# An encoder layer on one core: a new emission order around the output projection

## The chip, the cores and the metric

The kernel runs on one core of one Trainium2 chip. The metric is the device time of one execution in microseconds (us), the median of several runs. Before the change it is 1085.55 us (three runs, 1084.59 to 1087.48).

## The reference, cut to what matters

```python
def hybrid_mixer(u, w_in, ..., w_out):
    qa, ka, va, ga, za, qs, ks, vs = jnp.split(u @ w_in, SPLITS, axis=-1)
    ...
    o_a = o_f + o_b                       # gated linear attention, 4 heads, two directions
    o_a = o_a * lax.rsqrt(jnp.mean(o_a * o_a, axis=-1, keepdims=True) + NORM_EPS)
    o_a = (o_a * gla_norm).reshape(B, L, 512) * jax.nn.silu(ga)     # the output gate
    o_s = banded_window_gqa(qs, ks, vs, sink, rel_table)            # 8 heads, |i-j| <= 128
    return jnp.concatenate([o_a, o_s], axis=-1) @ w_out             # the output projection

h = h + rmsnorm(hybrid_mixer(rmsnorm(h, g1), ...), g2)
h = h + rmsnorm(jnp.square(jax.nn.relu(rmsnorm(h, g3) @ w_up)) @ w_down, g4)
```

There are 1024 tokens of width 1024, all in float32, and the feed-forward width is 4096.

## The kernel before, in words

Products are built from a high and a low part of each float32 factor (three matmuls hi*hi, lo*hi, hi*lo), so TensorE does most of the work. Each weight tile is loaded as float32 (`raw`, two buffers), cast to its high part by ScalarE (L93), and VectorE subtracts to get the low part (L196).

The program is a list of steps. The string ORDER is split into tokens, and a loop emits the instructions of one step per token. The framework then schedules: from the emission order, which acts as priority, it makes a fixed instruction list for each engine and each DMA queue and puts semaphore waits in. An engine executes its list strictly in that order. Moving a token therefore moves instructions on all lists, and a waiting instruction holds whatever stands behind it.

The steps that matter here are these.

- `gHh`, a gate step (`ga_half`, `proj_ga`): the gate of linear-attention head H for token half h. TensorE does 24 matmuls into the bank `pin` (L222: `uth,wh` x8, `uth,wl` x8, `utl,wh` x8), ScalarE takes the silu (L647, which needs another activation table than the exp of the attention), VectorE multiplies with the head's output (L649; that output `otr` is loaded by L648 on ScalarE's queue), and SyncE's queue stores four blocks into `otd` of the four tiles of that half (L651). A head's weights are fetched when the head before it in the list is done, so one head's two halves share one fetch.
- `S`, one attention step (`swa_step`) of 16; step u handles a block of 128 queries for one of two key heads. TensorE transposes the four heads' probabilities (`ppt`, L171), computes the next step's logits (`pl`, L545 and L546) and multiplies with the values (`pvo`, L579 to L583). VectorE casts and splits each transpose (L95, L571), adds the bias and takes a minimum on each logits bank (L548), then scales (L562). ScalarE does the exp (L551), and the copy of `pvo` (L585) that VectorE's L586 completes. Steps 2n and 2n+1 complete `otd` of tile n. `pl` and `pvo` share two banks of PSUM; so do `ppt` and `pzt` below.
- `Wk`, `wk` (`fetch_wo`): load, cast and split the k-th 128 rows of w_out (L752 for k < 4, in two halves by L756 for k >= 4; L93; L196).
- `Mn` (`wout_mm`): the output projection of tile n (128 tokens). It loads `otd[n]` (L801), casts (L802), splits (L803) and does 48 matmuls into two banks `pm` (L810: 32 with the high part of the activations, L815: 16 with the low part).
- `Nn` (`wout_norm`): squares of `pm` (L823), the root on GpSimd (L180, L181), scaling (L830), the residual (L832; the row of x is loaded by L820 on ScalarE's queue), squares again (L835), the root, and the second scaling (L839) into the tile `tb`.
- `Tn` (`wout_tr`): eight transposes of `tb` (`pzt`, L171), copied out by ScalarE (L858, L860) and VectorE (L861).

The list of one attention step, since both parts of the change turn on it:

```python
def swa_step():
    ...
    if u + 1 < 16:
        units[u + 1].load()
    for i in range(4):
        units[u].trans(i)
        if u + 1 < 16:
            units[u + 1].logits(i)
    units[u].pv()
    if u + 1 < 16:
        units[u + 1].norm()
```

After the output projection come the feed-forward products (L994, then L1223) to the end of the kernel.

Of the kernel before, what the change touches and what calls it, by code (L numbers as in the profile page):

```python
# [20 lines left out]
S = 1024  # L21
# [51 lines left out]
ORDER = (  # L73
# [4 lines left out]
)  # L78


# [1227 lines left out]
```

## Time and profile before

| | |
|---|---|
| median of three runs | 1085.55 us |
| the profiled execution | 1088.56 us |
| its span, first to last instruction | 1086.8 us |
| TensorE busy | 1048.9 us, 97% |
| VectorE busy | 744.0 us, 68% |
| ScalarE busy | 525.5 us, 48% |
| mean share of the 16 DMA engines in use | SyncE's queue 32.2%, GpSimd's 11.6%, ScalarE's 5.1% |

The profile comes from one execution. Times in the views are us from the start of its span. A timeline row gives the start, the length, the engine, the line, the operation, `out<-in`, the shapes, a count, and in brackets the idle time ahead of it with what ended that. PEclk is the clock granted to TensorE, where 1.00 is 2.4 GHz and 0.50 is 1.2 GHz. Matmul rows overlap by their pipelining, so pitches are taken between starts.

### The profile page before, as it was taken

To read this page: it belongs to the slowest core of one execution; us is meant where nothing else is said; L and a number is where in the kernel's file an instruction comes from. 1 tells how busy PE (TensorE), PEld (TensorE's weight loads), DVE (VectorE), ACT (ScalarE), POOL (GpSimd) and SP (SyncE) were. 2 spreads that over 40 slices of the span, in tenths; PEclk is the share of its full clock that TensorE was granted. 3 is DMA by queue.
4 is the path that set the end of the run, shared out by engine and by line. 5 is a ranking of instruction groups with operands and counts; after the bars stand their busy time and mean duration, and the time that the engine had idled before them with its cause. 6 is when DMAs were issued, how large, how long until landed. Compare 5 with 4: busy or idle time off the path is not lost.

```text
span 1086.8 us, 13683 instructions
## 1 busy us (share of the span) xinstructions
PE 1048.9 (97%) x4950; PEld 858.0 (79%) x4950; DVE 744.0 (68%) x1165; ACT 525.5 (48%) x890; POOL 161.4 (15%) x246
## 2 busy tenths in 40 slices
PE   7999999999997999989999999999999999999996
PEld 5787788888885878768888888888778888888885
DVE  7659458799887767798665666564479764547564
ACT  5565324424766444466555555554444334345342
POOL 4211012111211111111221212112100000004002
PEclk9999999999998999999999999999999999999999
DMA  7355443613666432546563544537982333345522
GB/s 227 111 159 173 131 115 84 143 40 93 190 171 162 122 121 84 160 152 207 177 191 116 177 143 148 172 119 238 392 325 97 98 97 97 116 136 193 194 97 97
DMA packets 138805, 164.82 MB, mean 152 GB/s; under 512 B 17473, under 2 KB 94273, under 8 KB 138738
## 3 DMA queue, kind: packets, MB, share of 16 engines
q1 hardware_dynamic: 108626, 108.36, 32.2%
q0 software_dynamic: 22560, 37.76, 11.6%
q10 hardware_dynamic: 7552, 17.83, 5.1%
q8 instruction: 39, 0.64, 0.2%
q14 instruction: 28, 0.23, 0.1%
HBM read 111.47 MB, written 52.45 MB: 151 GB/s over the span
## 4 chain that ended last, share of the span: by engine, by line
PE 81%; DVE 9%; ACT 3%; issue 3%; DMA 3%; POOL 1%; SPq 0%; ACTq 0%; DVEq 0%; POOLq 0%
PE pa L994 16%; PE pa L1223 14%; PE pin L222 11%; PE pc L994 8%; PE pb L1223 6%; PE pc L1223 6%; PE pm L810 4%; PE pb L994 4%; PE pkv L222 2%; PE ppt L171 1%; PE pm L815 1%; PE pl L545 1%; DMA wd<-in_w_down_dram 1%; PE pkv L692 1%; PE pl L546 1%
## 5 line engine op out<-in xcount | busy, mean ns | idle before, releaser
L1223 PE MATMUL pa<-r 128*128 128x512 f32 x768 | 175.1, 389 | 0.8 <-DVE r L1163 0.8
L1223 PEld LDWEIGHTS pa<-r 128*128 128x128 f32 x768 | 144.0, 188 | 31.4 <-DVE r L1163 1.6
L1162 DVE TENSOR_TENSOR r<-ra,r 128x1024 fp32r<-128x1024 f32 x56 | 68.5, 1223 | 106.7 <-ACT r L1160 105.3
L1160 ACT CAST r<-ra 128x1024 fp32r<-128x1024 f32 x56 | 58.9, 1053 | 165.9 <-PE pa L1223 94.1
L994 PE MATMUL pa<-th,r 128*128 128x512 f32 x384 | 102.3, 389 | 0.7 <-ACT sn L1009 0.7
L994 PEld LDWEIGHTS pa<-th,r 128*128 128x128 f32 x384 | 72.0, 188 | 16.0 <-ACT sn L1009 1.1
L222 PE MATMUL pin<-uth,wh 128*128 128x512 f32 x256 | 70.9, 400 | 0.0
L1223 PE MATMUL pb<-r 128*128 128x512 f32 x288 | 69.7, 390 | 0.0
L222 PE MATMUL pin<-uth,wl 128*128 128x512 f32 x256 | 69.4, 396 | 0.0
L1223 PE MATMUL pc<-r 128*128 128x512 f32 x288 | 69.2, 389 | 0.0
L810 PE MATMUL pm<-wo,b 128*128 128x512 f32 x256 | 67.5, 403 | 1.5 <-ACT b L802 1.5
L222 PE MATMUL pin<-utl,wh 128*128 128x512 f32 x256 | 66.9, 392 | 0.0
L1163 DVE TENSOR_TENSOR r<-wd,r 128x1024 fp32r<-128x1024 f32 x52 | 63.4, 1219 | 3.8 <-ACT r L1161 3.8
L1223 PEld LDWEIGHTS pb<-r 128*128 128x128 f32 x288 | 53.9, 188 | 11.9 <-DVE r L1163 0.7
L1223 PEld LDWEIGHTS pc<-r 128*128 128x128 f32 x288 | 54.1, 188 | 11.2
L180 POOL TENSOR_SCALAR cst<-cst 128x1 f32<-128x1 f32 x16 | 12.1, 754 | 323.6 <-ACT wd L1185 288.7
L1068 DVE TENSOR_TENSOR r<-su,r 128x1024 fp32r<-128x1024 f32 x32 | 39.0, 1220 | 28.9 <-ACT r L1067 28.9
L1161 ACT CAST r<-wd 128x1024 fp32r<-128x1024 f32 x52 | 54.6, 1050 | 5.4 <-DMA wd<-in_w_down_dram 5.4
L810 PEld LDWEIGHTS pm<-wo,b 128*128 128x128 f32 x256 | 47.5, 192 | 11.3 <-ACT b L802 2.4
L222 PEld LDWEIGHTS pin<-utl,wh 128*128 128x128 f32 x256 | 47.8, 188 | 9.7
L1002 ACT ACTIVATE ar<-ar 128x512 f32<-128x512 f32 x42 | 26.6, 632 | 56.3 <-DVE ar L1013 56.3
L222 PEld LDWEIGHTS pin<-uth,wl 128*128 128x128 f32 x256 | 47.0, 188 | 8.4
(282 smaller groups left out, 2136.3 us busy)
## 6 DMA issues: line engine op xcount, KB each, us to landing
ra<-hss SPq DMA_DIRECT2D x32, 512.0 KB, 3.6
wd<-in_w_down_dram SPq DMA_DIRECT2D x28, 512.0 KB, 9.3
hss<-ar POOLq DMA_DIRECT2D x54, 256.0 KB, 5.0
ra<-hsx SPq DMA_DIRECT2D x24, 512.0 KB, 3.8
hsx<-ar POOLq DMA_DIRECT2D x47, 256.0 KB, 2.9
ra<-in_w_up_dram SPq DMA_DIRECT2D x16, 512.0 KB, 4.1
rb<-in_w_up_dram SPq DMA_DIRECT2D x16, 512.0 KB, 5.9
raw<-in_w_in_dram SPq DMA_DIRECT2D x14, 512.0 KB, 4.6
```

Source lines behind the costliest of these rows:

```text
L171: nc.tensor.transpose(dst_bank[:, i * 128:(i + 1) * 128], s, ident)
L180: nc.gpsimd.tensor_scalar(r, ss, more, EPS, op0=ALU.add, op1=ALU.add)
L222: nc.tensor.matmul(p[:, cs], lhsT=a[:, kt, :], rhs=b[:, kt, cs], start=k == 0, stop=k == 23)
L810: nc.tensor.matmul(pm[c], lhsT=OTH[:, kt, :], rhs=w_[kt][:, sl], start=(w_ is woh and kt == 0), stop=False)
L994: nc.tensor.matmul(ps_, lhsT=a[:, kt, :], rhs=b[:, kt, :], start=p in (1, 2, 5) and n == 0 and kt == 0, stop=n == 2 and kt == 3, skip_grou ...
L1002: nc.scalar.activation(x_, x_ if src is None else src, AF.Relu)
L1068: late.append(lambda: nc.vector.tensor_sub(d[1], src, d[0]))
L1160: nc.scalar.copy(sd[0], ra[n % 2])
L1161: nc.scalar.copy(td[0], src)
L1162: nc.vector.tensor_sub(sd[1], ra[n % 2], sd[0])
L1163: nc.vector.tensor_sub(td[1], src, td[0])
L1223: nc.tensor.matmul(banks[t], lhsT=sd[a][:, c * 512 + t * 128:c * 512 + t * 128 + 128], rhs=td[b][:, c * 512:c * 512 + 512], start=p in (1, ...
```

## The change

Only the end of ORDER is written anew. No instruction is added or removed.

```diff
         "Q1 F11 E2 V2 C20 C21 R2 S S B20 B21 E3 V3 F21 F20 C30 C31 R3 S S g00 B30 B31 F31 g01 S F30 S W0 S "
-        "g11 g30 W1 g31 g10 W2 W3 g20 w4 w5 S S w6 g21 S w7 M0 N0 M1 T0 S N1 M2 T1 N2 M3 T2 N3 M4 T3 S S M5 "
-        "N4 T4 M6 N5 T5 N6 M7 T6 "
+        "g10 g30 W1 g11 W2 W3 S g20 w4 w5 g31 w6 S w7 g21 M0 N0 M1 T0 S N1 M2 T1 S N2 M3 T2 S N3 M4 T3 S M5 N4 "
+        "T4 M6 N5 T5 N6 M7 T6 "
```

Gates of the first half (g10, g30, g20) now come ahead of the others where the weights allow. Before M0 there are two attention steps in place of three, and of the steps behind M0 one stands behind each of T0, T1, T2 and T3, where one stood behind T0 and two behind T3.

The first place is TensorE's list from the last eight matmuls of the last gate step (g21) to the first of M0. Before:

```order
L222 MATMUL pin<-utl,wh 128x512 x8
L579 MATMUL pvo<-s_89 128x512
L545 MATMUL pl<-s_88 128x384
L546 MATMUL pl<-s_88,qz 128x384
...
L171 MATMUL ppt<-cst,s_85 128x128 x6
L545 MATMUL pl<-s_88 128x384
L546 MATMUL pl<-s_88,qz 128x384
L810 MATMUL pm_3075<-wo,b_3062 128x512
L171 MATMUL ppt<-cst,s_85 128x128 x3
L810 MATMUL pm_3075<-wo,b_3062 128x512 x4
```

and with the change:

```order
L222 MATMUL pin<-utl,wh 128x512 x8
L545 MATMUL pl<-s_88 128x384
L546 MATMUL pl<-s_88,qz 128x384
L171 MATMUL ppt<-cst,s_85 128x128 x3
L545 MATMUL pl<-s_88 128x384
L546 MATMUL pl<-s_88,qz 128x384
L171 MATMUL ppt<-cst,s_85 128x128 x3
L579 MATMUL pvo<-s_89 128x512
...
L545 MATMUL pl<-s_88 128x384
L546 MATMUL pl<-s_88,qz 128x384
L810 MATMUL pm_3011<-wo,b_2998 128x512 x16
```

Before, a part of an attention step and the whole of the next are spread between the matmuls of M0 and M1; now most of one step stands alone between g21 and M0, and M0 and M1 are 96 matmuls in one piece.

The second place is ScalarE's list from the silu of the last gate step to the first cast of M0's activations (L802). Before:

```order
L647 ACTIVATE g_517<-pin 128x512
L93 CAST wo<-raw 128x1024
L551 ACT_TABLE_LOAD
L551 ACTIVATE s_85,cst<-s_85,cst 128x384
L585 COPY s_531<-pvo 64x512
L557 ACTIVATE cst<-cst 128x4
L93 CAST wo<-raw 128x1024
L802 CAST b_3062<-b_3061 128x1024
```

and with the change:

```order
L820 DMA xb<-in_x_dram 128x1024
L647 ACTIVATE g_517<-pin 128x512
L551 ACT_TABLE_LOAD
L551 ACTIVATE s_85,cst<-s_85,cst 128x384
L93 CAST wo<-raw 128x1024
L551 ACTIVATE s_85,cst<-s_85,cst 128x384 x2
L93 CAST wo<-raw 128x1024
L551 ACTIVATE s_85,cst<-s_85,cst 128x384
L557 ACTIVATE cst<-cst 128x4
L585 COPY s_531<-pvo 64x512
L802 CAST b_2998<-b_2997 128x1024 x2
```

The load of x for the first tile (L820) has moved from ahead of the fourth w_out cast to here, and the last two w_out casts (w6, w7) and an attention copy (L585) now all stand between the last silu and the first cast of the projection.

The third place is SyncE's queue from the fetch of w3 (the last L752) to the load of the second tile's activations (`otd_524`); L756 fetches halves of w4 to w7, and L651 stores a gate's four blocks. Before:

```order
L752 DMA raw<-in_w_out_dram 128x1024
L756 DMA raw<-in_w_out_dram 64x1024
L651 DMA otd_523<-g_517 128x128
...
L756 DMA raw<-in_w_out_dram 64x1024 x2
...
L756 DMA raw<-in_w_out_dram 64x1024
L801 DMA b_3061<-otd_523 128x8x128
L756 DMA raw<-in_w_out_dram 64x1024 x2
L651 DMA otd_527<-g_517 128x128
...
L756 DMA raw<-in_w_out_dram 64x1024 x2
L801 DMA b_3061<-otd_524 128x8x128
```

and with the change:

```order
L752 DMA raw<-in_w_out_dram 128x1024
L756 DMA raw<-in_w_out_dram 64x1024 x4
L651 DMA otd_523<-g_517 128x128
...
L756 DMA raw<-in_w_out_dram 64x1024 x2
L651 DMA otd_527<-g_517 128x128
...
L756 DMA raw<-in_w_out_dram 64x1024 x2
L801 DMA b_2997<-otd_523 128x8x128
L801 DMA b_2997<-otd_524 128x8x128
```

The first activations (`otd_523`) stood ahead of the last four halves and now stand behind all eight.

## Rows read from the trace of the kernel before

**Rows 1.** The page's first part: busy time of TensorE and its share of the span.

```profile
PE 1048.9 (97%) x4950; PEld 858.0 (79%) x4950; DVE 744.0 (68%) x1165; ACT 525.5 (48%) x890; POOL 161.4 (15%) x246
```

**Rows 2.** Waits of TensorE, 309 to 348 us (us in total, times, longest).

```profile
PE pl L545 <- DVE s L586: 2.6, 1, 2.6
PE ppt L171 <- DVE s L571: 1.9, 1, 1.9
PE pl L545 <- DVE cst L548: 1.1, 1, 1.1
PE pm L810 <- ACT b L802: 1.1, 1, 1.1
```

**Rows 3.** Windows: length, busy us per engine, granted clock, DMA share, GB/s.

```profile
core 0: us, PE busy (x) PEld busy (x) DVE busy (x) ACT busy (x) POOL busy (x), PEclk, DMA share, GB/s
326.30:328.40 2.10, 0.21 (x1) 0.02 (x1) 2.10 (x4) 1.42 (x2) 0.00 (x0) 1.00 0.37 125
339.00:348.00 9.00, 6.71 (x24) 5.17 (x24) 5.92 (x17) 4.84 (x9) 1.30 (x3) 0.62 0.58 159
373.88:390.78 16.90, 16.36 (x85) 13.06 (x84) 13.92 (x32) 8.69 (x22) 2.12 (x4) 1.00 0.31 101
390.78:402.81 12.03, 11.52 (x54) 9.39 (x55) 6.44 (x8) 5.50 (x12) 1.40 (x3) 1.00 0.40 132
373.88:447.39 73.51, 71.53 (x352) 57.64 (x350) 54.45 (x98) 35.81 (x81) 9.84 (x18) 1.00 0.40 127
```

**Rows 4.** Timeline of ScalarE and its queue, and of SyncE's queue, 317 to 342 us.

```profile
317.61 0.46 SPq L752 DMA_DIRECT2D raw<-in_w_out_dram  x1
...
317.65 0.37 ACTq L820 DMA_DIRECT2D xb<-in_x_dram  x1
...
324.89 1.05 ACT L93 CAST wo<-raw 128x1024 fp32r<-128x1024 f32 x1 [4.98 <-DMA raw<-in_w_out_dram]
...
333.45 0.60 ACT L647 ACTIVATE g<-pin 128x512 f32<-128x512 f32 x1
333.95 1.04 ACT L93 CAST wo<-raw 128x1024 fp32r<-128x1024 f32 x1
335.01 1.28 ACT L551 ACT_TABLE_LOAD   x1
336.30 0.61 ACT L551 ACTIVATE s<-s,cst 128x384 f32<-128x384 f32 x1
```

**Rows 5.** DMA issues, 310 to 345 us: count, KB each, median us from issue to landing.

```profile
raw<-in_w_out_dram SPq DMA_DIRECT2D x8, 256.0 KB, 3.9
...
b<-otd SPq DMA_DIRECT2D x2, 512.0 KB, 8.9
...
xb<-in_x_dram ACTq DMA_DIRECT2D x1, 512.0 KB, 6.7
```

**Rows 6.** DMA issues of the whole execution, same columns.

```profile
raw<-in_w_out_dram SPq DMA_DIRECT2D x4, 512.0 KB, 4.3
```

**Rows 7.** Timeline of VectorE, 318 to 342 us.

```profile
318.12 0.68 DVE L586 TENSOR_TENSOR s<-pvo,s 64x512 f32<-64x512 f32 x1
...
320.16 0.69 DVE L649 TENSOR_TENSOR g<-g 128x512 f32<-128x512 f32 x1
...
331.65 1.21 DVE L196 TENSOR_TENSOR wo<-raw,wo 128x1024 fp32r<-128x1024 f32 x1
...
338.65 1.43 DVE L562 TENSOR_SCALAR s<-s,cst 128x384 f32<-128x384 f32 x4
340.00 0.55 DVE L95 CAST s<-ppt 128x384 fp32r<-128x384 f32 x1
...
341.47 0.54 DVE L95 CAST s<-ppt 128x384 fp32r<-128x384 f32 x1
```

**Rows 8.** Timeline of TensorE: end of g21, first matmul of M0, middle of M1.

```profile
331.42 2.00 PE L222 MATMUL pin<-utl,wh 128*128 128x512 f32 x8
...
343.20 0.79 PE L810 MATMUL pm<-wo,b 128*128 128x512 f32 x1 [1.06 <-ACT b L802]
...
364.10 6.30 PE L810 MATMUL pm<-wo,b 128*128 128x512 f32 x27
```

**Rows 9.** Waits of TensorE, 373 to 456 us, same columns as rows 2.

```profile
PE pzt L171 <- DVE tb L839: 1.5, 3, 0.5
```

**Rows 10.** Timeline of tile 3's N: its first squares and its last scaling.

```profile
405.39 0.64 ACT L823 ACTIVATE tb<-pm 128x512 f32<-128x512 f32 x1
...
413.41 1.28 DVE L839 SCALAR_TENSOR_TENSOR tb<-xb,cst,b 128x1024 f32<-128x1024 f32 x1 [2.98 <-POOL cst L181]
```

## The prediction

> **What bounds the kernel now.** I read the busy times first. TensorE works 97% of the span [rows 1], so nothing off TensorE pays by itself: the change can only move TensorE's idle time, or the time in which its clock is low. TensorE's list is the same before and after up to 309.1 us, and it has the same structure again from M6 on. So I read TensorE's waits between, in two stretches.
>
> The first is the end of the gates and the attention steps ahead of M0. Four waits end there, 2.6 + 1.9 + 1.1 + 1.1 = 6.7 us, and VectorE or ScalarE releases each [rows 2]. The windows then tell of the clock: in the 9 us from 339 it was 0.62 of full speed on average [rows 3], which costs 9.0 x 0.38 = 3.4 us. Idle time and low clock together are about 10 us, all that could be won there. The wait of 1.9 us starts with a transfer: w3 is issued at 317.61 and is cast only at 324.89, 7.3 us later, with ScalarE idle for 4.98 us and the load of x issued beside it at 317.65 [rows 4].
>
> The second stretch is the tiles. From tile 0's transposes (373.88) to tile 5's (447.39) TensorE is busy for 71.53 of 73.51 us [rows 3], and the wait for N's last scaling comes to 1.5 us in three places [rows 9]. Two us are all that lies there.
>
> **The change part by part.** No instruction is added or taken away, so the sum is of gaps and clock, and of nothing else.
>
> *Price of the pieces.* A projection matmul has a pitch of (6.30 - 0.40) / 26 = 0.227 us [rows 8]. From pzt0 to pzt1 TensorE does 50 projection matmuls and an attention step in 16.36 us; from pzt1 to pzt2 46 of the former alone in 11.52 us [rows 3]. A step costs 16.36 - 11.52 - 4 x 0.227 = 3.9 us. Its six value products take 6 x 0.227 = 1.4, which leaves 2.5 for four blocks of transposes and logits, 0.64 a block.
>
> *Gates.* The load of x is now behind w3 on ScalarE's list. I let w3 land in the 4.3 us that is the median of its four like [rows 6], not in 7.3: it comes at about 322. VectorE's split of it is the gap of 1.9 us; I estimate 0.9 is left of it. But another logits bank is waited for by what now stands earlier, which I price at the like wait, 1.1 [rows 2], and 0.4 for what I can't place between the bounds of nothing and 1.1. Gaps ahead of g21's end are then 2.4 where they were 1.9.
>
> *Attention ahead of M0.* One set of value products and two blocks now stand ahead of g21's end instead of behind: 1.4 + 2 x 0.64 = 2.6 us. So g21's end moves from 331.42 + 8 x 0.227 = 333.3 [rows 8] to 333.3 + 2.6 + 0.5 = 336.4. From there one chain leads to M0. ScalarE does the silu (0.60), the table load (1.28), one exp (0.61) and the cast of w6 (1.04) [rows 4], until 339.9; VectorE splits w6 (1.21) and casts the last transpose (0.55) [rows 7], until 341.6; five value products follow, at half the clock 5 x 0.45 = 2.3, until 343.9; then the copy of `pvo` on ScalarE, about 0.6, L586 (0.68) [rows 7], and a logits pair: M0 starts at about 346.4 instead of 343.20 [rows 8]. w7's cast and the first activations are waited for by nobody if they come before that.
>
> *M0 and M1.* They now stand in one piece: 96 x 0.227 = 21.8 us and about 2 us of low clock at its start, until 370.2. Deferred attention follows, 3.9 less two logits pairs of 0.35 that were done ahead of M0: 3.2. Tile 0's transposes come at 373.4, against 373.88: a gain of 0.4. Counted the other way, by gaps, the new stretch has 1.1 + 0.9 + 0.4 + 1.2 + 2.6 + 1.2 = 7.4 us of waits against 6.7 and the same loss of clock: a cost of 0.7. The two workings share their rows and differ in what they neglect, so I take the middle, +0.1, and both as bounds.
>
> *Tiles.* N of tile 0 takes 405.39 to 414.69, 9.3 us, in tile 3's undisturbed case [rows 10], and M1 behind it 10.9, so pzt0 doesn't begin to wait. Three tiles have an attention step beside them instead of two with the same total. A tile without a step waits some 0.5 us for N [rows 9], and one with a step waits for as little as nothing (pzt3 and pzt4 aren't among the three) or for the N chain that VectorE's 13.92 us of 16.90 [rows 3] hold up. I take +0.3, between -1.5 (all three waits gone) and +1.5 (as many again).
>
> **Sum:** 0.1 + 0.3 = +0.4 us. The profiled execution took 1088.56 us, its span 1086.8, the rest 1.76 around it; the median of the runs is 1085.55, 3.0 lower. A sum so small goes over as it is: 1089.0 on the profile's scale, and **1086.0 us** for the median. About 0.3%, or 3.3 us, is what a measurement can tell from no change.
>
> **The clock, weighed.** The row: a gap of 1.9 us (326.3 to 328.4) left the clock at 1.00, while the waits of 2.6, 1.1 and 1.1 us close behind each other brought it to 0.62 over the 9 us from 339 [rows 2, 3]. In the new list such waits still stand close together, so I keep the loss. The Trainium skill, "TensorE: Matmul & The Clock Gate", section "HAM oscillation — how this bites in real kernels", says that matmul groups with waits between them throw TensorE back to 1.2 GHz, which speaks against a gain here; by that the 3.4 us stay, and with an unthrottled stretch the sum would be 0.4 - 3.4 = -3.0.
>
> **The rivals.**
>
> *Faster: VectorE alone sets the stretch.* For it: VectorE's list from L586 at 318.12 holds three L586 (0.68), two scalings (1.43), eight block pairs (340.00 to 341.47: 1.47 each), five splits (1.21) and three L649 (0.69) [rows 7], 24.8 us; it ends at 342.9 if every transfer and ScalarE are ahead of it. M0 would start at 343.6, 2.8 sooner than in my chain, and with so few gaps the clock would not fall, 3.4 more [rows 3]. That is 0.4 - 6.2 = -5.8: about 1080 us. Against it: ScalarE's two casts and the silu in the chain above, and the three table switches there.
>
> *Slower: the transfers decide.* If w3 takes 7.3 us as before [rows 4], its split ends at 327.2; w5 uses the buffer that this frees, and lands 7.3 later, at 334.5; cast (1.04) and split (1.21) end at 336.8, and w7's load takes that buffer. SyncE's queue has the first activations behind all of w7, where before four halves stood behind them: issued at about 338, landing 8.9 us later [rows 5], at 346.9, cast at 348. M0 is then 1.6 later than in the forecast, and for the longer pause I estimate a further 2 us of half clock: 0.4 + 3.6 = +4.0, about 1090 us. It decides from the point where tile 0's activations land after about 345.3. For it: the DMA landings of 7.3, 6.7 and 8.9 us in just this stretch [rows 4, 5], and that x's load (512 KB) now comes in the middle of these. Against it: the eight halves of w_out took 3.9 in the median [rows 5]. The Trainium skill, "DMA: Bandwidth & Descriptors", section "Issuing engines are not separate DMA queues", says that loads of different engines run on the same 16 engines and interleave: x's load would then not be made free by its place on ScalarE's queue, only moved, and the time that w3 gains would be lost by w6, w7 or the activations.
>
> *Nothing but a shift.* Gains and losses of under 1 us cancel; this is the forecast's own case.
>
> **How the numbers follow.** Forecast 0.46 (within 3.3 us of no change, with the bounds of the terms: -0.4 or +0.7, and -1.5 to +1.5, so -1.9 to +2.2). Faster rival 0.30, since VectorE's list sums to nearly my start and ScalarE's waits are only estimated. Slower rival 0.24. The range reaches both rivals' ends with an allowance of 1 us above: 1080 to 1091. The forecast's own range is 1083.6 to 1087.8.
>
> **What would show it.** Right: M0's first matmul near 346 on the trace, 10 us or more of it behind g21's last matmul; w3's cast near 322; waits before M0 of about 7 us; a clock near 0.6 in the 9 us around M0's start; 73 to 75 us from pzt0 to pzt5. Wrong towards faster: M0 at 343 to 344 and a clock of 1.00 throughout. Wrong towards slower: w7's load issued after 336, tile 0's activations landing after 345.3, and a wait of M0 for L802 of over 2 us. The prediction is wrong in its order of causes if the tiles, and not the stretch ahead of M0, hold most of the difference.

## The result, and the profile after

The changed kernel takes 1092.36 us (median of six runs, 1090.02 to 1093.34) against 1085.68 us for the kernel before: a ratio of 1.006, 95% interval 1.0048 to 1.0072. It is 6.7 us slower; the forecast was +0.4 us, and the time lies above the range. The profiled execution's span is 1091.6 us, 4.8 over the one of before, and TensorE's busy time in it answers to [rows 1]:

```profile
PE 1051.7 (96%) x4950; PEld 859.5 (79%) x4950; DVE 747.0 (68%) x1165; ACT 526.2 (48%) x890; POOL 161.3 (15%) x246
```

The matmuls are the same; at half clock each counts as busy for longer (a value product for 0.63 us at 343.45, for 0.39 at 329.50).

TensorE's waits in the changed kernel, from 309 to 352 us (the counterpart of [rows 2]), and from 352 to 480 us:

```profile
PE pvo L579 <- DVE s L95: 3.0, 1, 3.0
PE pm L810 <- ACT b L802: 1.6, 1, 1.6
PE pl L545 <- DVE s L586: 1.4, 1, 1.4
PE pl L545 <- DVE cst L548: 1.2, 2, 0.8
PE ppt L171 <- DVE s L571: 0.3, 1, 0.3
```

```profile
PE pzt L171 <- DVE tb L839: 7.6, 7, 5.2
...
```

The waits of the first stretch make 7.5 us, where they were 6.7. Among those of the tiles is the 5.2 us of the last tile, which is in both kernels.

The windows of the changed kernel (columns as in [rows 3]): the 9 us from 339, the 27 us from 339, the stretch from 309.09 to tile 0's transposes, and from there to tile 7's.

```profile
339.00:348.00 9.00, 4.68 (x10) 2.61 (x10) 6.96 (x15) 4.44 (x10) 1.32 (x3) 0.58 0.96 227
...
339.00:366.00 27.00, 21.30 (x74) 16.20 (x75) 10.94 (x20) 7.92 (x16) 2.56 (x5) 0.75 0.43 105
...
309.09:373.45 64.36, 56.78 (x246) 44.22 (x245) 42.12 (x90) 31.20 (x56) 8.26 (x13) 0.89 0.62 155
...
373.45:477.76 104.31, 96.31 (x473) 77.67 (x472) 84.12 (x148) 54.76 (x120) 17.10 (x28) 1.00 0.39 124
```

The last three of these for the kernel before, whose last tile's transposes came at 474.35:

```profile
339.00:366.00 27.00, 24.71 (x111) 19.89 (x111) 21.22 (x53) 11.95 (x28) 4.53 (x8) 0.87 0.45 107
...
309.09:373.88 64.79, 57.95 (x266) 45.99 (x265) 49.62 (x114) 34.19 (x66) 9.71 (x15) 0.95 0.61 155
...
373.88:474.35 100.47, 92.78 (x452) 74.88 (x450) 75.84 (x124) 50.99 (x110) 14.46 (x25) 1.00 0.40 128
```

Three readings. Tile 0's transposes come at 373.45 against 373.88, as early as before, but an attention step has left this stretch: from there to tile 7's transposes takes 104.31 against 100.47 us, 3.8 more, and the idle time in it is almost the same (8.0 against 7.7). So the moved step costs behind M0 what it should, 3.9 us, and the stretch ahead of M0 and under M0 and M1, relieved of it, gained only 0.4. What ate that is idle time and clock: over 27 us from 339 the clock was 0.75, a loss of 27 x 0.25 = 6.8 us, against 27 x 0.13 = 3.5. The other 1.4 of the 4.8 us lie behind tile 7's transposes (613.84 against 612.45 us); further executions of both kernels took 612.1 to 613.7 us there, so that is scatter.

Where M0 stood, by the timelines of ScalarE, SyncE's queue and VectorE:

```profile
336.35 0.60 ACT L647 ACTIVATE g<-pin 128x512 f32<-128x512 f32 x1 [2.55 <-PE pin L222]
...
342.62 0.68 DVE L649 TENSOR_TENSOR g<-g 128x512 f32<-128x512 f32 x1
...
338.16 1.15 SPq L801 DMA_DIRECT2D b<-otd  x2
343.33 1.80 SPq L651 DMA_DIRECT2D otd<-g  x4
...
348.28 1.04 ACT L802 CAST b<-b 128x1024 fp32r<-128x1024 f32 x1 [2.31 <-DMA otd<-g]
```

M0's first matmul follows at 349.38. I had worked out 338 for the issue of tile 0's activations in the slower rival, and it is 338.16. But the bracket on the last row names another transfer: by it ScalarE stood idle until a store of the last gate (`otd<-g`) had landed, not until the load (`b<-otd`) had. When this load landed, the trace does not have.

### The profile page after: what moved, and what is told of

Same layout as the page of the kernel before. It is cut to its first block, busy times and chain, and to the rows that moved or that the text cites. A ratio compares the mean times of both kernels' runs of the same rounds, so it can differ in the third digit from the quotient of the medians.

```text
span 1091.6 us, 13677 instructions
## 1 busy us (share of the span) xinstructions
PE 1051.7 (96%) x4950; PEld 859.5 (79%) x4950; DVE 747.0 (68%) x1165; ACT 526.2 (48%) x890; POOL 161.3 (15%) x246
## 4 chain that ended last, share of the span: by engine, by line
PE 81%; DVE 8%; DMA 4%; ACT 3%; issue 3%; POOL 1%; SPq 0%; ACTq 0%; DVEq 0%; POOLq 0%
PE pa L994 15%; PE pa L1223 14%; PE pin L222 11%; PE pc L994 8%; PE pb L1223 6%; PE pc L1223 6%; PE pm L810 4%; PE pb L994 3%; PE pkv L222 2%; PE ppt L171 2%; DMA wd<-in_w_down_dram 1%; PE pm L815 1%; PE pl L545 1%; PE pkv L692 1%; PE pl L546 1%
```

## The experiments

They are told in the order in which they ran. All ratios are against runs of the kernel before on the same chip, whose median varied from 1085.0 to 1086.6 us between jobs. Two chips were in use, so between jobs the ratios compare better than the times.

**The two halves of the change, apart.** The gates alone (e1):

```diff
-g11 g30 W1 g31 g10 W2 W3 g20 w4 w5 S S w6 g21 S w7 M0
+g10 g30 W1 g11 W2 W3 g20 w4 w5 S S g31 w6 g21 S w7 M0
```

> The new order of the gates, with the attention steps where they stood before (two after w5, one after g21, one after T0, two after T3). Theory A (the loss of 6.7 us comes from the place of the attention steps: one of them stands alone between g21 and M0, with VectorE as its bound, and the clock falls behind it): within 2 us of the kernel before, M0's first matmul at 343 to 345 us, mean clock over 339 to 375 us of 0.88 or more. Rival B (the loss comes from the transfers that the gates' order moves: w4 to w7, x and tile 0's activations): 4 us or more slower than before, with a wait of M0 for L802 of over 1 us.

Measured 1090.97 us, ratio 1.0052 (1.0038 to 1.0065); M0 starts at 351.76. No matmul waited for L802 there; attention's waits (3.5 + 2.5 + 1.4 + 0.8 us) stood ahead of M0. The steps alone (e2):

```diff
-g20 w4 w5 S S w6 g21 S w7 M0 N0 M1 T0 S N1 M2 T1 N2 M3 T2 N3 M4 T3 S S M5
+S g20 w4 w5 w6 S g21 w7 M0 N0 M1 T0 S N1 M2 T1 S N2 M3 T2 S N3 M4 T3 S M5
```

> The new places of the attention steps (two ahead of M0, one after each of T0 to T3), with the gates in the order of before. Theory A: slower than before by 5 to 8 us, like the changed kernel. Rival B: within 2 us of before.

Measured 1091.6 us, ratio 1.0060 (1.0048 to 1.0073); M0 at 348.45, after a wait for L802 of 2.5 us. By the time, the first run is B's and the second is A's; neither theory has both, since each half alone costs nearly all of it. That suggests something common behind both.

**The load of tile 0's activations, sooner.** L801 of tile 0 is emitted by a step of its own (e3):

```diff
-g31 w6 S w7 g21 M0
+g31 w6 P S w7 g21 M0
```

> The changed kernel, but the load of tile 0's activations is emitted between w6 and w7 instead of behind w7. Rival B (that load holds M0): M0's wait for L802 (1.6 us) goes, M0 starts near 347.7 instead of 349.4, and with a shorter stretch of low clock the kernel is 2.5 to 4 us faster than the changed one, so 3 to 4 us slower than before. Theory A (VectorE's list and the clock): the 1.6 us go at most, and the time is 0 to 1.6 us below the changed kernel.

Measured 1091.78 us, ratio 1.0060 (1.0047 to 1.0072). The load was issued at 336.11, 2.0 sooner, and landed 5.1 us later, at 341.2; its cast still started at 348.50. In this run the load did not hold the cast: B's mechanism falls as long as the slot named below is shared.

**The second attention step ahead of w6** (e7).

```diff
-g20 w4 w5 g31 w6 S w7 g21 M0
+g20 w4 w5 S g31 w6 w7 g21 M0
```

> The changed kernel with the second attention step moved from behind w6 to behind w5, so that g31 and g21 stand beside it on TensorE and nothing of attention is left alone between g21 and M0. Theory A: the waits between g21 and M0 for the attention step (0.4 + 3.0 + 1.4 us) go or come earlier beside gate matmuls, M0 starts by 346 us, and the kernel is 3 us or more faster than the changed one. Rival B: M0 then waits for the transfers instead, L802 takes the place of the waits with 4 us or more, and the time stays within 2 us of the changed kernel.

Measured 1091.22 us, ratio 1.0055 (1.0043 to 1.0068). The load was issued at 333.73, and the cast came at 348.86, 15 us later. M0's wait for it grew to 3.1 us, where B had said 4 or more, and the time was B's. But the bracket of this cast names a store of the last gate again, not the load: the cast waits for something else.

**Both kernels profiled again**, to see how steady the clock is.

> The kernel before, profiled once more, since its profiled execution (1088.56 us) lies 3 us over the median of its runs and lost 3.4 us to a low clock in the 9 us from 339. Theory C (that loss of clock is not in every execution; most keep the clock up at M0's start): a span near 1083.5 us and a clock of 0.95 or more from 339 to 348. Rival (the loss is in every execution, and the 3 us are elsewhere or come from profiling): a clock of 0.6 to 0.7 there again.

> The same again, to see whether the clock around M0's start differs between executions of one kernel. Theory C: 0.95 or more from 339 to 348 in at least one of these two. Rival: 0.6 to 0.7 in both.

> The changed kernel, profiled once more. Theory C: the waits of 3.0, 1.4 and 1.6 us come again within 0.3 us each, and the low clock between 339 and 360 with them (6 us or more lost), since the attention step alone leaves TensorE idle in every execution. Rival: the waits come again, but the clock stays up, and the span is 4 us shorter than 1091.6.

The kernel before: span 1087.5 and 1083.3 us, clock 0.62 and 0.72 from 339 to 348, so theory C falls: over 309 to 366 us it was 0.94 each time, 57 x 0.06 = 3.4 us, in all three executions. What differs is the idle time from 309.09 to tile 0's transposes: 6.8, 4.7 and 4.3 us; my execution was the worst of three. The changed kernel: span 1088.5 us, waits the same within 0.6 us, and the clock over 309 to 366 us 0.94 instead of 0.88. So its loss by the clock is 6.8 in one execution and 3.4 in the other, between what theory C and its rival said; its idle time is 7.6 and 8.0.

**Filler** (e8). A token ahead of M0 emits 17 matmuls of w5's and w6's parts into a free bank; their result is not used.

```diff
-w7 g21 M0
+w7 g21 D M0
...
+pd = bank("ga", "pd")
+for k_ in [5] * 14 + [6] * 3:
+    nc.tensor.matmul(pd, lhsT=woh[k_][:, 0:128], rhs=woh[k_][:, 0:512], start=True, stop=True)
```

> The changed kernel with 17 added matmuls, whose result is not used, among the attention step that stands alone between g21 and M0 (14 need only w5's parts, 3 only w6's). They fill the wait of 3.0 us ahead of the value products. Theory A (the clock falls because TensorE has nothing to do there): the clock stays at or near 1.00 through M0, which wins back about 5 of the 6.8 us lost between 339 and 375, less at most 1.5 us by which the added matmuls hold the step up: 3 to 5 us faster than the changed kernel. Rival B (the transfers and VectorE's list set M0's start, and the clock costs little): within 1 us of the changed kernel or slower.

Measured 1091.01 us, ratio 1.0046 (1.0034 to 1.0059): between the two forecasts, and not clear of the changed kernel's interval. The wait of 3.0 us was gone, and M0's wait had grown in its place. The waits, and the cast:

```profile
PE pm L810 <- ACT b L802: 4.5, 1, 4.5
...
348.44 1.04 ACT L802 CAST b<-b 128x1024 fp32r<-128x1024 f32 x1 [4.81 <-DMA otd<-g]
```

The clock was 0.96 over the 9 us from 339, but 0.87 over the 27 us: the loss came later. M0 started at 349.54, as without the filler. The attention step did not set M0's start, then; L802 did. In all variants so far L802 came 3 to 6 us behind the first issue of the last gate's stores, and its bracket named `otd<-g`. The code says why. The high and low parts of the activations lie in the slot G3 (`b3`), and so do the gates' products (`gst`) that L651 stores:

```python
g3 = slot("G3", 8, F32, "g3")
...
gst = [g3(4, 512), g3(6, 512)]
...
b3 = slot("G3", 8, F32R, "b3")
...
wb["OTH"], wb["OTL"] = b3.three(0, 8, 128), b3.three(4, 8, 128)
```

The first cast of the projection must wait until the last store of the last gate has read that slot.

**A buffer of its own** (e9). Tile 0's parts go into the two `wl` buffers, which the last gate's matmuls leave free; the transposes' copies (`zf`), which used these, take them from T0 on.

```diff
+wb["OH0"] = [slot("wl", 4, F32R, "oh", 2).three(0, 8, 128) for _ in range(2)]
...
-OTH, OTL = wb["OTH"], wb["OTL"]
+OTH, OTL = wb["OH0"] if n == 0 else (wb["OTH"], wb["OTL"])
```

> The changed kernel, but tile 0's high and low activations (L802, L803) get a buffer of their own instead of the slot in which the gates keep the products that they store. Theory G (in every variant so far the first L802 came 3 to 6 us behind the issue of the last gate's stores, wherever the load of its activations stood: it waits until those stores have read that slot, not for the load): L802 starts before 346 us, M0's wait for it (1.5 to 1.6 us) goes, M0 starts 1.5 us or more sooner, at about 347, and the time is 1.5 to 3 us below the changed kernel. Rival B (the load of tile 0's activations, issued at 338, sets it): L802 stays at 347.5 or later and nothing changes by more than 1 us.

Measured 1088.39 us, ratio 1.0015 (1.0004 to 1.0025), 0.0045 (4.9 us) below the changed kernel's, more than G's 1.5 to 3 us. Yet in the profiled execution the details were B's: L802 at 347.71, and now the bracket names the load.

```profile
347.71 1.04 ACT L802 CAST oh<-b 128x1024 fp32r<-128x1024 f32 x1 [1.57 <-DMA b<-otd]
```

Issued at 339.16, it had taken 8.5 us. So the load stands right behind the slot as a second bound, and in that execution the clock was 0.75 from 339 to 366 again. It took 1091.58 us, 3.2 over the median of its kernel, so no trace shows how the others won their time.

The own buffer with the filler (e10):

> The same own buffer together with the 17 filler matmuls, after which M0's wait for L802 was 4.5 us. Theory G: that wait falls below 1 us, M0 starts at 345 to 346 instead of 349.5, the clock stays above 0.9 from 339 to 357, and the time is 4 to 7 us below the changed kernel, close to the kernel before. Rival B: the wait stays above 3 us and the time within 1.5 us of the filler run (1091.0).

Measured 1085.37 us, ratio 0.9999 (0.9986 to 1.0012): the changed order with both is as fast as the kernel before. M0 starts at 345.08, 4.5 us sooner than with the filler alone, and its wait is 1.1 us, just above G's limit. The cast and the window of this run:

```profile
343.98 1.04 ACT L802 CAST oh<-b 128x1024 fp32r<-128x1024 f32 x1 [0.57 <-DMA b<-otd]
...
339.00:366.00 27.00, 25.79 (x111) 20.25 (x111) 13.59 (x22) 10.34 (x20) 3.00 (x6) 1.00 0.58 147
```

In the changed kernel theory G holds: 0.0047 lies between this run and the filler alone, and they differ by the buffer only (and by what the scheduler made of it).

**The last gate sooner**, with the shared slot (e11, `w4 w5 g31 g21 w6 S w7 M0`).

> The changed kernel with its last gate step (g21) right behind g31, ahead of w6 and of the second attention step, and the gates' slot as it was. Theory G: the multiply of the last gate and its stores come sooner (before 338 us) and no longer hold L802; M0 starts before 347 and the time is 2 to 5 us below the changed kernel. Theory A (an attention step that stands alone ahead of M0 costs its own waits and the clock, whatever the gate does): no gain, or a loss of up to 2 us, since more of the attention step stands alone.

Measured 1090.0 us, ratio 1.0034 (1.0022 to 1.0046): 0.0026 better than the changed kernel, in G's range. But M0 started at 349.52, not before 347: the stores were issued from 338.32, the load of the activations behind them at 340.95, and L802 waited for that load until 348.43. Under this gate order the two bounds lie close together. This execution took 1092.49 us, 2.5 over the median of its kernel.

**The control: the kernel before with the own buffer** (e12).

> The kernel before with the own buffer for tile 0's activations, as a control. Theory G: there the last gate's stores were issued at 335 and L802 had no idle time ahead of it for them, so nothing moves: within 1.5 us of the kernel before. If it is 2 us or more faster, the slot also held the kernel before, and its share in the difference is smaller than the own buffer's gain in the changed kernel.

Measured 1083.22 us, ratio 0.9973 (0.9963 to 0.9983): faster than both kernels, and against my first expectation. The slot had held the kernel before too, by the order. With the buffer free, the scheduler put L802 ahead of w6's cast on ScalarE's list; before, it stood behind it, at 342.11. M0 starts at 338.26, without a wait for L802:

```profile
337.70 0.44 PE L545 MATMUL pl<-s 128*128 128x384 f32 x1 [2.65 <-DVE s L586]
...
338.26 0.74 PE L810 MATMUL pm<-wo,oh 128*128 128x512 f32 x2
```

and the window of the 27 us from 339:

```profile
339.00:366.00 27.00, 26.98 (x133) 22.11 (x132) 23.89 (x57) 12.96 (x30) 5.11 (x8) 1.00 0.54 136
```

TensorE is busy for 26.98 of these 27 us, and the clock stays at 1.00.

The control also limits what the slot explains. With the own buffer in both kernels, in the same job, the change still costs 1.0015 - 0.9973 = 0.0042, some 4.6 us; with the shared slot it was 0.0060. Measured so, the slot's share in the difference between the two kernels is 0.0018, about 2 us. Where the rest lies the two traces show: from 309.09 us to tile 0's transposes TensorE is idle for 7.8 us at a mean clock of 0.89 in e9, and for 3.9 us at 1.00 in e12.

**What is left with the slot free.** Four more: the changed order with the own buffer and the load ahead of w6 on GpSimd's queue (e13); the gates alone (e14) and the steps alone (e15), each with the own buffer; and the kernel before with it, its three late steps behind T0, T1 and T2 (e16).

> The changed kernel with the own buffer, and the load of tile 0's activations issued ahead of w6 and on GpSimd's queue, so that neither the slot nor the place behind w7 on SyncE's queue holds the first L802; no filler. Theory G with the load as second bound (in the own-buffer run L802 waited for that load instead, 339.2 to 347.7): L802 starts before 343, M0's wait for it is under 0.5 us, M0 starts at 346 to 347.5, where VectorE's L586 sets it, and the time is 1 to 3 us below the own-buffer run (1088.4). Rival C (the clock alone decides what is left): M0's start comes sooner, but the clock falls as before in the attention step that stands alone, and the time stays within 1 us of 1088.4.

> The gates' new order with the attention steps where they were before, and the own buffer. Without it this was 6.0 us slower than before. If the slot is all that the gates' order costs, the time comes to within 1.5 us of the kernel before with the own buffer (1083.2); if the order costs by itself (its waits of 3.5 + 2.5 us for attention ahead of M0), it stays 3 us or more above that.

> The attention steps' new places with the gates in the order of before, and the own buffer. Without it this was 6.6 us slower than before. If the slot is all that the steps' places cost, within 1.5 us of 1083.2; if the step that stands alone ahead of M0 and the thinner cover cost by themselves, 3 us or more above that.

> The kernel before with the own buffer and its front as it was, but the three attention steps behind M0 placed one after each of T0, T1 and T2 instead of one after T0 and two after T3. Tells whether the spread between the tiles costs by itself: if it doesn't, within 1 us of 1083.2; if each tile with a step beside it waits longer for its norm, 1 to 2 us above.

| order | slot shared | own buffer |
|---|---|---|
| before | 1 | 0.9973 (0.9963 to 0.9983) |
| gates alone | 1.0052 | 0.9993 (0.9985 to 1.0002), 1085.24 us |
| steps alone | 1.0060 | 0.9985 (0.9976 to 0.9994), 1084.05 us |
| both (the change) | 1.0060 | 1.0015 (1.0004 to 1.0025) |
| both, load early | 1.0060 | 1.0011 (1.0000 to 1.0022), 1086.44 us |
| before, steps spread | | 1.0001 (0.9991 to 1.0011), 1085.94 us |

With the slot free, either half alone costs 0.0012 to 0.0020, 1 to 2 us, instead of six. The two together cost 0.0042, with the load early 0.0038, and with the filler 0.0026: in the whole change something more than the slot holds M0, and the runs do not settle how it divides between the late load, the step that stands alone and the clock. e15 came out within the first of its two expectations; e14, 2.0 us above 1083.2, lies between its two, nearer the first. In e14 M0 starts at 340.32, 11.4 us sooner than in e1, where no matmul had waited for L802: there the slot acted through the order that the scheduler made. In e15 M0 starts at 335.79, ahead of the attention copy at 343.47: its matmuls again lie between those of the attention step. e13 missed in its detail: M0 started at 339.94, sooner than forecast, because the scheduler mixed M0 with the attention step there also; it still waited 4.0 us for the load, issued on GpSimd's queue at 330.52 and cast at 338.85, 8.3 us later. Its time, 2 us below that of the own-buffer run but 0.0004 by the ratios with overlapping intervals, doesn't settle how much the load's place is worth. e16 missed by a little: spreading the steps cost 0.0028, 3 us, where I expected up to 2. Its profiled execution shows 102.76 us from tile 0's to tile 7's transposes with TensorE busy for 92.77, against 100.22 and 92.19 with the steps where they were: idle time of 10.0 against 8.0. It took 1088.5 us, 2.6 over the median of its kernel, and it is a further 3.3 us behind the control's at tile 0's transposes, ahead of which no token was moved.

## Why the prediction was wrong

*What bounds the kernel; price of the pieces.* Right. A step priced at 3.9 us lengthened the tiles by 3.8 us.

*Gates.* Right. w3 was cast at 322.52, forecast 322; g21's matmuls ended at 336.3, forecast 336.4. The wait for w3's split was 1.0 to 1.9 us in three executions before and 0.3 and 0.9 in two after.

*Attention ahead of M0: the step that failed.* I wrote that w7's cast and the first activations are waited for by nobody if they come before 346.4. L802 came at 348.28, and M0 started at 349.38, 3.0 us later than worked out. Of these, 1.6 us are M0's wait for L802. The other 1.4 are the chain itself, mis-sized: its terms as written add up to about 345.5, not 346.4, and the value products, which began at 341.69 (worked out: 341.6), lasted until 345.4, with a logits pair among them, 3.7 us where I had 2.3. The chain I followed ran over VectorE's list, and it did have waits on it (3.0 + 1.4 us), but filling them moved M0 by nothing. The chain that I didn't see has the last gate in it: its silu ended at 336.95, its multiply stands in VectorE's list behind attention's blocks and came only at 342.62, its stores were issued from 343.33, and they released the slot that the first cast writes. In the kernel before the last gate's stores were issued at 335.04. With the slot free and the waits filled (e10), M0 started at 345.08. How much of the whole 6.7 us this step cost stays open: freeing the slot won 0.0045 to 0.0047 in the changed kernel and 0.0027 in the one before, and 0.0042 of the difference is there without it. That the change puts the last gate behind everything else was in its string of tokens; that this gate holds a buffer of the projection was in the code, and I read neither `b3` nor `gst` for it.

*The list as a consequence.* I took M0's and M1's 96 matmuls in one piece as a thing that the change does. The runs show it as the scheduler's answer to the slot in at least the steps-alone order: with the own buffer the same tokens mix M0 and the attention step (e15). In the changed order it is not so: with the own buffer alone M0 stays in one piece (e9), and where it is mixed (e13) TensorE still waits 4.0 us for the load.

*The same loss of clock.* Wrong in size. Idle time from 309.09 to tile 0's transposes is 6.8, 4.7 and 4.3 us in three executions before, 7.6 and 8.0 after: 2.5 more on average. The clock's loss is 3.4 in all three before, 6.8 and 3.4 after, 1.7 more on average. That is 4.2 of the 4.2 us between the mean spans (1085.9 and 1090.05 us). The medians of the timed runs lie 6.7 apart. The other 2.5 us come from which executions were profiled: these took 1087.6 and 1091.8 us on average, against medians of 1085.7 and 1092.4, and two of the three of before (1088.56 and 1089.27 us) were longer than all 86 timed runs of that kernel, of which the longest took 1088.23. The timed runs are listed with a mean clock each; span x (1 - clock), an estimate, gives 10.4 us lost in the mean of six runs after, and 8.3 to 9.3 in the four jobs that list the kernel before. So by this estimate the clock accounts for 1 to 2 of the 6.7 us, and the rest is time at full clock. The sentence from the Trainium skill, "TensorE: Matmul & The Clock Gate", section "HAM oscillation — how this bites in real kernels", pointed the right way: in the profiled execution the waits between matmul groups went with a clock of 0.58 over 9 us from 339 and 0.66 over the next 9, and where they were filled and the slot freed (e10), and in the control (e12), it was 1.00. My own row for the clock was no rule: waits of 2.6 + 1.0 + 0.5 us came with a loss of 3.4 us (the third execution of before), waits of 2.6 + 2.0 + 0.6 with none (e16).

*M0 and M1; tiles.* Tile 0's transposes at 373.45 against 373.4 looks like a hit and is none: I had put 3.2 us of deferred attention ahead of them, and it lies behind: M0's lateness cancelled it. The term of +0.3 for the tiles' own waits held (8.0 against 7.7 us of idle time). That tile 0's transposes came as forecast is luck, then: two errors of some 3 us against each other.

*The rivals.* The slower one had the sign and the place: M0 waits for L802, with a price of +4.0 us, and the mean profiled spans differ by 4.2; its own sign, a wait for L802 of over 2 us, came out at 1.6. While the slot was shared it had the wrong cause: an earlier load did nothing (e3). With the slot free the load becomes the bound (8.5 us in e9), so this rival may have a part in the 0.0042 that is left; e13 does not settle it.

## What to carry to other kernels

Before moving a step, list the buffers that its tiles share with the step ahead of it in the program: whoever writes a reused slot first waits for the last reader of the old tile, and a store that drains it is such a reader. When a step is moved to the end of a phase, follow it through the in-order lists to its last transfer, and ask who needs its memory. When two edits that should be independent each cost the whole difference, look for one resource that both delay. And when a repair wins time, apply it to the kernel before as well: here the own buffer won 0.0045 in the changed kernel, but 0.0027 in the one before, so less than half of it was due to the change.

## What the runs showed of the hardware

I had not expected the clock to vary so: nearly the same string of waits (7.6 and 8.0 us of idle time) cost 6.8 us in one execution of the changed kernel and 3.4 in the other. In e10 (where the filler counts as work) and e12, with 2.1 and 3.9 us of idle time in that stretch, it cost nothing; in the kernel before, 4.3 us of idle time still cost 3.4. With 5.4 us (e16) it cost nothing, and with 3.8 us (e14) 57 x 0.06 = 3.4: the sum of the idle time does not tell the clock, and the runs do not show what does. Two kernels that differ by one buffer (e12 and the one before) differ by 3.4 us of clock in the profiles, and by 2.9 us in the ratio of their times; but by the mean clocks of their timed runs in that job (0.9936 and 0.9923) only some 1.4 us of this are the clock.

A load of 512 KB took 8.5 us from SyncE's queue (e9) and 8.3 us from GpSimd's (e13) in nearly the same stretch, from issue to the start of the cast that waited for it; another queue made it no faster.
